# Hybrid decoder layer: the forgetting queries and keys as four pairs by seven products behind the heads, token-major values at the heads' seams

## The chip, the cores and the metric

The kernel runs on one core of a Trainium2 chip. The core's engines run side by side, each through its own list of instructions: TensorE (PE; its weight loads are PEld), VectorE (DVE), ScalarE (ACT), GpSimd (POOL), and SyncE (SP), on whose queue all DMAs are issued. The metric is the device time of one execution in microseconds (us).

## The reference, cut to what matters

The layer works on 1024 tokens of width 1024. A first normalisation is followed by one wide projection, whose columns feed two groups of heads: four mLSTM heads (queries and keys through a causal convolution, values, an output gate, two scalar gates) and eight forgetting-attention heads (queries, keys, values, one gate). Then come cross-attention into 256 memory tokens and an MLP with a squared ReLU.

```python
h = rmsnorm(x, ln1[l])
z = h @ w_in[l]
ml_qk, ml_v, ml_o, ml_i, ml_f, fx_q, fx_k, fx_v, fx_f = jnp.split(z, splits, axis=-1)
ml_qk = jax.nn.silu(causal_conv(ml_qk, ml_conv_w[l], ml_conv_b[l]))
...
mh = mlstm_chunkwise(mq, mk, mv, ig, lf)
...
fx_out = forgetting_attention(fq, fk, fv, flf).reshape(B, S, FX_W)
x = x + jnp.concatenate([ml_out, fx_out], axis=-1) @ w_out[l]
x = x + cross_attention(...)
...
```

The part that the change rewrites is `fx_q` and `fx_k`: h (1024 tokens by 1024) times 512 columns of weights for the queries and 512 for the keys.

## The kernel before, in words

**Number format.** Every matrix product is made in float32 by three matmuls (`mm3`, lines 186 to 188): each operand is cut into a high and a low part by `split` (lines 134 and 135: a ScalarE copy for the high part, a VectorE subtraction for the low one; lines 137 and 138 where a factor goes in), and low times high, high times low and high times high add up in one bank.

**Order of the work.** The program is written stage after stage, but a planner lays out each engine's list: it takes the instructions by the order in which the program has them, passes over one whose operands or buffers are not there yet by its own estimate, and takes a later one instead. Tiles have names (`w2("p")` is the name `r_p`, `act`, `w4`, `z4`, `wr` for raw weights, `wh` and `wl` for cut ones; `sc`, `tp`, `mm`, `m2`, `ov` for the eight banks of PSUM) and a number of buffers each: act 7, w4 5, z4 2, wr 2, wh and wl 3, r_p 2, r_c 2; sc 3, tp 2, the others 1. `mm()` gives out banks by the list `banks`. Where an order is wanted exactly, `in_order()` chains the instructions of an engine; the attention's slots do so.

**The stages that matter here.**
1. `first_values` makes the first half of the mLSTM values together with the gates while x arrives. The squares' sums (line 234) give the factors `rcol` of the norm; `first_sink` evicts the banks with them (lines 138 and 379).
2. `token_major(a["w_mv"], mv_sink, (1,), ...)` makes the second half of the values in eight tiles of 128 tokens by 256 columns, 24 matmuls each. Among the tiles stand `row_first` (the factors as a row across the partitions, by a transpose at line 249 and two DMAs through `rowd`) and `gate_rows` (transposes at lines 457 and 462, scans at 463 and 467); `gate_cols` follows.
3. `ml_project(hd)` for each of the four mLSTM heads: `conv_silu` of the key (a projection of two halves of 24 matmuls into two banks, evicted with the norm row at line 507, four taps at lines 510 and 512, tanh at 514, the product at 515, in two `z4` tiles that line 505 begins); `fx_project(0, hd)`; the carried state (lines 535 to 549); `conv_silu` of the query; `fx_project(1, hd)`; the output gate `og` (line 672).
4. `fx_project(which, n)` is a plain projection: 128 columns of queries or keys, 48 matmuls of 128x512, evicted with the norm row (line 641), cut and stored to the scratch `fqk` (lines 644 and 645).
5. `ml_head(hd, ...)` is the head itself: scores into `sc`, weights by exp (line 586), mask (588), product (589), cut, and the value product into `ov`; its closing steps run as a generator (`closing`) between the steps of the next projection. Four heads follow one another; head 3 is the last.
6. Forgetting attention: `fx_load` loads a head's queries and keys from `fqk` into `stacks` (whose memsets are line 696); `slot` issues one step each of scores (lines 734 and 735), maximum, exp, scaling and value product. Thirteen slots of scores lead (`LEAD_`), and behind them `token_major(a["w_fv"], fv_sink, ...)` makes the forgetting values in 16 tiles. From then on each value slot also takes work from `filler()` (memory keys and values, the first part of the output projection), at `RATE` planned units a slot.

## Time and profile before

| what | value |
|---|---|
| device time, median of three runs | 1511.57 us (1509.03 to 1512.43) |
| profiled execution, first to last instruction | 1509.2 us (no other time of its own is given) |
| TensorE busy | 1493.0 us, 7806 matmuls |
| weight loads busy | 1263.7 us |
| VectorE busy | 1122.7 us |
| ScalarE busy | 757.7 us |
| GpSimd busy | 528.7 us |

The page gives for each engine the time in which it ran an instruction. Matmuls overlap their neighbours in these records, so that single durations are longer than the step from one to the next; a stretch of the span, divided by the matmuls in it, gives the step. A row of waits names the waiting instruction, what released it, the time in all, the number of times and the longest.

### The profile page before, as it was taken

How to read it: one execution, taken by the hardware profiler on the slowest of the kernel's cores; microseconds unless marked ns; L12 is line 12 of the kernel's file. 1: busy time of each engine (PE TensorE's matmuls, PEld its weight loads, DVE VectorE, ACT ScalarE, POOL GpSimd, SP SyncE). 2: the span in 40 equal slices, each digit the busy share in tenths (PEclk: the TensorE clock that was granted, in tenths of full speed). 3: DMA queues.
4: the chain of work that ended last, by engine and by line, in shares of the span. 5: the costliest groups of instructions: out<-in, count | busy, mean ns of one | idle time of the engine just before them, and what ended most of it. 6: DMA issues, size and time to landing. Idle time of an engine off the chain costs nothing.

```text
span 1509.2 us, 22358 instructions
## 1 busy us (share of the span) xinstructions
PE 1493.0 (99%) x7806; PEld 1263.7 (84%) x7806; DVE 1122.7 (74%) x1803; ACT 757.7 (50%) x1440; POOL 528.7 (35%) x545
## 2 busy tenths in 40 slices
PE   9999999999999999999999999999999999999997
PEld 9988888889899888788988878888888888888887
DVE  7766676664788875667767899989996678787765
ACT  7324343334688764566654467566664521122134
POOL 1003030414365441623300044454544365553312
PEclk9999999999999999999999999999999999999999
DMA  6322333435777877853354447676678677776623
GB/s 243 115 79 95 98 108 126 132 129 153 247 261 256 284 248 246 271 169 126 128 182 159 147 155 279 235 261 248 217 273 292 264 279 279 279 272 251 247 88 112
DMA packets 124276, 303.04 MB, mean 201 GB/s; under 512 B 13810, under 2 KB 28460, under 8 KB 117252
## 3 DMA queue, kind: packets, MB, share of 16 engines
q1 hardware_dynamic: 124164, 301.62, 57.3%
q8 instruction: 61, 1.00, 0.3%
q14 instruction: 51, 0.42, 0.1%
HBM read 202.75 MB, written 98.82 MB: 200 GB/s over the span
## 4 chain that ended last, share of the span: by engine, by line
PE 90%; DMA 4%; DVE 3%; ACT 1%; issue 1%; POOL 1%; POOLq 0%; DVEq 0%; SPq 0%; ACTq 0%
PE tp L186 8%; PE tp L187 8%; PE tp L188 8%; PE sc L186 6%; PE sc L188 6%; PE sc L187 6%; PE mm L186 5%; PE m L188 5%; PE m L186 5%; PE m L187 5%; PE mm L188 5%; PE mm L187 5%; PE ov L801 2%; PE ov L186 2%; PE ov L187 2%; PE ov L188 2%
## 5 line engine op out<-in xcount | busy, mean ns | idle before, releaser
L186 PE MATMUL tp<-act,wl 128*128 128x512 f32 (+1 forms) x440 | 172.6, 392 | 0.0
L187 PE MATMUL tp<-act,wh 128*128 128x512 f32 (+1 forms) x440 | 172.1, 391 | 0.0
L188 PE MATMUL tp<-act,wh 128*128 128x512 f32 (+1 forms) x440 | 171.8, 392 | 0.0
L135 DVE TENSOR_TENSOR wl<-wr,wh 128x1024 fp32r<-128x1024 f32 (+2 forms) x99 | 131.4, 1327 | 27.0 <-ACT wh L134 26.7
L134 ACT ACTIVATE wh<-wr 128x1024 fp32r<-128x1024 f32 (+2 forms) x99 | 99.8, 1008 | 85.7 <-PE tp L188 32.7
L186 PE MATMUL mm<-act,wl 128*128 128x512 f32 (+1 forms) x332 | 124.8, 376 | 2.6 <-DVE r_c L138 2.1
L188 PE MATMUL mm<-act,wh 128*128 128x512 f32 (+1 forms) x332 | 124.1, 374 | 0.0
L187 PE MATMUL mm<-act,wh 128*128 128x512 f32 (+1 forms) x332 | 123.8, 373 | 0.0
L186 PE MATMUL m<-act,wl 128*128 128x512 f32 (+1 forms) x308 | 113.8, 369 | 0.6 <-DVE wl L135 0.6
L188 PE MATMUL m<-act,wh 128*128 128x512 f32 (+1 forms) x308 | 113.8, 369 | 0.0
L187 PE MATMUL m<-act,wh 128*128 128x512 f32 (+1 forms) x308 | 113.7, 369 | 0.0
L188 PE MATMUL sc<-act,wh 128*128 128x512 f32 (+1 forms) x280 | 105.6, 377 | 0.0
L187 PE MATMUL sc<-act,wh 128*128 128x512 f32 (+1 forms) x280 | 105.6, 377 | 0.0
L186 PE MATMUL sc<-act,wl 128*128 128x512 f32 (+1 forms) x280 | 105.6, 377 | 0.0
L1612 POOL TENSOR_TENSOR z<-wr 128x256 f32<-128x256 f32 x56 | 52.9, 966 | 131.8 <-DMA wr<-w_ff2q 126.7
L188 PEld LDWEIGHTS tp<-act,wh 128*128 128x128 f32 x440 | 82.7, 188 | 19.0
L186 PEld LDWEIGHTS tp<-act,wl 128*128 128x128 f32 x440 | 82.7, 188 | 18.5
L187 PEld LDWEIGHTS tp<-act,wh 128*128 128x128 f32 x440 | 82.7, 188 | 18.2
L134 ACT ACTIVATE wh<-z 128x1024 fp32r<-128x1024 f32 (+1 forms) x54 | 55.5, 1027 | 81.8 <-POOL z L1612 62.3
L135 DVE TENSOR_TENSOR wl<-z,wh 128x1024 fp32r<-128x1024 f32 (+1 forms) x54 | 77.7, 1439 | 11.4 <-ACT wh L134 11.4
L134 ACT ACTIVATE w<-wr 128x768 fp32r<-128x768 f32 (+3 forms) x35 | 28.0, 801 | 107.4 <-PE tp L186 33.0
L186 PEld LDWEIGHTS mm<-act,wl 128*128 128x128 f32 x332 | 62.7, 189 | 14.2 <-DVE r_c L138 2.6
(734 smaller groups left out, 4387.2 us busy)
## 6 DMA issues: line engine op xcount, KB each, us to landing
act<-right SPq DMA_DIRECT2D x49, 1024.0 KB
right<-w SPq DMA_DIRECT2D x56, 256.0 KB
wr<-w_ff2q SPq DMA_DIRECT2D x28, 512.0 KB
right<-r_d SPq DMA_DIRECT2D x49, 256.0 KB
right<-r_e SPq DMA_DIRECT2D x49, 256.0 KB
act<-fqk SPq DMA_DIRECT2D x48, 256.0 KB
wr<-w_in SPq DMA_DIRECT2D x20, 512.0 KB
wr<-w_ff SPq DMA_DIRECT2D x20, 512.0 KB
```

The lines of the kernel that those rows point to most:

```text
L134: s.activation(hi, src, AF.Copy)
L135: return v.tensor_tensor(out=lo, in0=src, in1=hi.bitcast(F32), op=ALU.subtract)
L186: nc.tensor.matmul(ps, w[1], x[0], start=first, stop=False, skip_group_check=more)
L187: nc.tensor.matmul(ps, w[0], x[1], start=False, stop=False, skip_group_check=more)
L188: nc.tensor.matmul(ps, w[0], x[0], start=False, stop=last, skip_group_check=more)
L801: nc.tensor.matmul(self.ov[:, c0:], self.fv[:, self.j], t[:, c0:], start=self.j == 0 and t is self.p[1], stop=self.last and t is self.p[0])
L1612: g.tensor_tensor(out=o, in0=x, in1=y, op=op)
```

## The change

`fx_project` is gone from the heads' seams. The eight mLSTM value tiles of the second half and the 16 tiles of forgetting values, which stood ahead of the heads and behind the first scores, go there instead, four ahead of the carried state and four behind the query's convolution (`token_units`, called by `ml_project` for heads 1, 2 and 3; head 0 has none). `row_first` and `gate_rows` stand without tiles around them.

Behind the heads, the query and key projections are made as four pairs of one query tile and one key tile. Each pair is a 2 by 2 product of blocks (query and key columns by the two halves of the depth, against the two halves of the depth by the two halves of the tokens), made with seven block products in place of eight. Their right sides are four blocks or sums of blocks (`t1` to `t4`) of the normed input, made from x once by `first_rights` and `last_rights`, and the blocks of h themselves; the left sides are made from the weights by `left_in`. `InPair.run` makes a product (four k by three matmuls of 128x512) and evicts or adds, and stores to `fqk`. `in_jobs` is the order of the products. The query and key quarters of heads 0 and 2 (before: 1 and 3) now lie in an `act` tile.

In the attention's lead, the forgetting values are gone, and the slots take work from `filler()`, at `WARM` planned units a slot; `RATE` goes from 4.6 to 4.0.

```diff
--- before.py
+++ after.py
...
@@ -485,19 +488,17 @@
                 load(decay[sign, p_], cut[p_].bitcast(F32))
-    def token_major(w_src, sink, cs=(0, 1), between={}):
-
-        for c in cs:
-            ws = [both(weights(w_src[c, i]), lambda t: t.rearrange("p (k c) -> p k c", k=4)) for i in range(2)]
-            for t in range(8):
-                if t in between:
-                    between[t]()
-                hf, tt = divmod(t, 4)
-                ps = mm()[:, 0:256]
-                for k in range(KT):
-                    x = both(h[hf], lambda z: z[:, k, tt * P : (tt + 1) * P])
-                    mm3(ps, x, both(ws[k // 4], lambda z: z[:, k % 4]), k == 0, k == KT - 1)
-                sink(t, c, ps)
+    def token_units(w_src, sink, c):
+        ws = [both(weights(w_src[c, i]), lambda t: t.rearrange("p (k c) -> p k c", k=4)) for i in range(2)]
+        for t in range(8):
+            hf, tt = divmod(t, 4)
+            ps = mm()[:, 0:256]
+            for k in range(KT):
+                x = both(h[hf], lambda z: z[:, k, tt * P : (tt + 1) * P])
+                mm3(ps, x, both(ws[k // 4], lambda z: z[:, k % 4]), k == 0, k == KT - 1)
+            sink(t, c, ps)
+            yield
     def conv_silu(n, hi, lo):
         w = weights(a["w_in"][n])
@@ -634,16 +635,6 @@
     fqk = dram.tile([2, 2, 4, P, T], F32, name="fqk")
-    def fx_project(which, n):
-        w = weights(a["w_in"][12 + 4 * which + n])
-        for _, hf, ps in proj(w, h, 1):
-            lo = w2("p")
-            v.scalar_tensor_tensor(out=lo, in0=ps, scalar=1.0 if which else FXD ** -0.5, in1=row[:, hf * TH : hf * TH + TH], op0=ALU.mult, op1=ALU.mult)
-            hi = w2("p", dt=F32R)
-            split(hi, lo.bitcast(F32R), lo)
-            load(fqk[which, 0, n, :, hf * TH : hf * TH + TH], hi.bitcast(F32))
-            load(fqk[which, 1, n, :, hf * TH : hf * TH + TH], lo)
-
     fvd = dram.tile([FXH, P, 8, 2 * FXD], F32, name="fvd")
     def fv_sink(t, c, ps):
@@ -653,18 +644,20 @@
     closing = iter(())
-    def ml_project(hd):
-        qk = quarters(F32R) if hd % 2 else [w4(dt=F32R) for _ in range(4)]
+    def ml_project(hd, tiles=iter(())):
+        qk = quarters(F32R) if hd % 2 == 0 else [w4(dt=F32R) for _ in range(4)]
         q, k = qk[:2], qk[2:]
         weighed = weigh(hd)
         yk = conv_silu(MLH + hd, *k)
         next(closing, None)
-        fx_project(0, hd)
+        for _ in range(4):
+            next(tiles, None)
         next(closing, None)
         state = carried(hd, yk, *weighed)
         next(closing, None)
         yq = conv_silu(hd, *q)
-        fx_project(1, hd)
+        for _ in range(4):
+            next(tiles, None)
         sums = carry(hd, q, yq, *state)
         og = w4()
         for _, hf, ps in proj(weights(a["w_in"][8 + hd]), h, 1):
@@ -675,17 +668,187 @@
     banks[:] = ["tp", "m2", "tp", "sc", "mm", "sc", "sc"]
     turn[0] = 0
-    token_major(a["w_mv"], mv_sink, (1,), {2: row_first, 4: gate_rows})
+    row_first()
+    gate_rows()
     gate_cols()
     banks[:] = ["mm", "tp", "m2", "tp"]
     with tc.issue_after(last_sum.ins):
         mem_prepare()
+    mv_tiles = token_units(a["w_mv"], mv_sink, 1)
+    fv_tiles = [token_units(a["w_fv"], fv_sink, c) for c in range(2)]
     ready = ml_project(0)
     for hd in range(MLH):
         closing = ml_head(hd, *ready)
         next(closing)
         if hd < MLH - 1:
-            ready = ml_project(hd + 1)
+            ready = ml_project(hd + 1, (mv_tiles, *fv_tiles)[hd])
+    I_RIGHT = {}
+    for c, hf, k0 in (("11", 0, 0), ("21", 0, 4), ("22", 1, 4)):
+        I_RIGHT[c] = [both(h[hf], lambda t: t[:, k0 + k]) for k in range(4)]
+    raw_x = act(F32)
+    t1, t2 = act(), act()
+    I_RIGHT["t1"] = [(t1[:, k], t1[:, 4 + k]) for k in range(4)]
+    I_RIGHT["t2"] = [(t2[:, k], t2[:, 4 + k]) for k in range(4)]
+    I_RIGHT["t3"] = [both(h[1], lambda t: t[:, k]) for k in range(4)]
+    I_RIGHT["t4"] = [(t[:, :TH], t[:, TH:]) for t in (w4(dt=F32R) for _ in range(4))]
+    def gain(n):
+        return vec[:, VEC["ln1"] + n :][:, 0:1]
+    def x_part(k, hf, tag):
+        t = w2(tag)
+        load(t, a["x"][:, 4 + k, hf * TH : hf * TH + TH])
+        return t
+    def first_rights():
+        for hf in range(2):
+            load(raw_x[:, 4 * hf : 4 * hf + 4], a["x"][:, 0:4, hf * TH : hf * TH + TH])
+        for k in range(4):
+            x, y = raw_x[:, k], raw_x[:, 4 + k]
+            z = x_part(k, 1, "pc"[k % 2])
+            s.activation(y, y, AF.Copy, scale=gain(k))
+            v.scalar_tensor_tensor(out=x, in0=x, scalar=gain(k), in1=y, op0=ALU.mult, op1=ALU.subtract)
+            s.activation(I_RIGHT["t1"][k][0], x, AF.Copy, scale=-1.0)
+            v.scalar_tensor_tensor(out=I_RIGHT["t1"][k][1], in0=x, scalar=-1.0, in1=I_RIGHT["t1"][k][0].bitcast(F32), op0=ALU.mult, op1=ALU.subtract)
+            s.activation(z, z, AF.Copy, scale=gain(4 + k))
+            g.tensor_tensor(out=x, in0=z, in1=x, op=ALU.add)
+            sub(y, z, y, g)
+            split(*I_RIGHT["t3"][k], y)
+    def last_rights():
+        for k in range(4):
+            x = raw_x[:, k]
+            split(*I_RIGHT["t2"][k], x)
+            z = x_part(k, 0, "pc"[k % 2])
+            v.scalar_tensor_tensor(out=x, in0=z, scalar=gain(4 + k), in1=x, op0=ALU.mult, op1=ALU.subtract)
+            split(*I_RIGHT["t4"][k], x)
+    I_NAMES = {1: "11", 2: "21", 5: "t1", 6: "t2", 3: "22", 7: "t3", 4: "t4"}
+    i_cycle = ("sc", "mm", "tp", "sc", "m2", "tp", "sc", "ov")
+    def i_bank():
+        turn[0] += 1
+        return ps_tile(i_cycle[turn[0] % 8])
+    IP = 4
+    in_jobs = [(0, 1), (0, 5), (0, 2), (0, 3), (1, 1), (1, 5), (1, 2), (0, 6), (1, 3), (0, 7), (0, 4), (1, 6), (1, 7)]
+    for p_ in range(2, IP):
+        in_jobs += [(p_, 1), (p_ - 1, 4)] + [(p_, i) for i in (5, 2, 6, 3, 7)]
+    in_jobs.append((IP - 1, 4))
...
+    def left_in(p_, group):
+        if group == 0:
+            in_raws[p_] = [sb("wr", [P, 1024], 2) for _ in range(2)]
+            for raw, n in zip(in_raws[p_], (16 + p_, 12 + p_)):
+                load(raw, a["w_in"][n])
+        r2, r1 = in_raws[p_]
+        x11, x12, x21, x22 = r1[:, :TH], r1[:, TH:], r2[:, :TH], r2[:, TH:]
+        if group == 0:
+            t = z4()[:, :T].bitcast(F32R)
+            h22, l22 = t[:, :TH], t[:, TH:]
+            split(h22, l22, x22)
+            in_cuts[p_, 4] = both((h22, l22), lambda t: t.rearrange("p (k c) -> p k c", k=4))
+        hi, lo = (sb(t, [P, 1024], 3, F32R) for t in ("wh", "wl"))
+        split(hi, lo, (r1, r2, r1)[group])
+        if group == 0:
+            by = g if p_ else v
+            by.tensor_tensor(out=x21, in0=x21, in1=x22, op=ALU.add)
+            sub(x22, x21, x11, by)
+            sub(x12, x12, x22, by)
+            sub(x11, h22.bitcast(F32), x22, by)
+            by.tensor_tensor(out=x11, in0=x11, in1=l22.bitcast(F32), op=ALU.add)
+        for e in range(2):
+            in_cuts[p_, ((1, 2), (5, 6), (7, 3))[group][e]] = both((hi, lo), lambda t: t[:, e * TH : e * TH + TH].rearrange("p (k c) -> p k c", k=4))
+    class InPair:
...
+        def run(self, i, l):
+            r = I_RIGHT[I_NAMES[i]]
+            at_ = {1: "a", 2: "a", 5: "c", 3: "c", 6: "b", 7: "b", 4: "b"}[i]
+            if i in (1, 5, 6):
+                setattr(self, at_, i_bank())
+            ps = getattr(self, at_)
+            for k in range(4):
+                mm3(ps, both(l, lambda t: t[:, k]), r[k], i in (1, 5, 6) and k == 0, k == 3, True)
+            u = self.u
+            if i == 1:
+                self.p1 = w2("p")
+                s.activation(self.p1, ps, AF.Copy)
+            elif i == 2:
+                v.tensor_tensor(out=self.room("11", "a", "y"), in0=ps, in1=self.row_of("11"), op=ALU.mult)
+                self.done("11")
+            elif i == 5:
+                self.add(self.room("22", "e"), ps, self.p1)
+            elif i in (6, 3):
+                if "12" not in u:
+                    self.add(self.room("12", "b", "f"), ps, self.p1)
+                else:
+                    self.add(u["12"], ps, u["12"])
+                    self.scale("12")
+            elif i == 7:
+                self.add(u["22"], ps, u["22"])
+                self.scale("22")
+            elif i == 4:
+                u["21"] = self.p1
+                self.add(u["21"], ps, u["21"])
+                self.scale("21")
+        def scale(self, c):
+            g.tensor_tensor(out=self.u[c], in0=self.u[c], in1=self.row_of(c), op=ALU.mult)
+            self.done(c)
+        def done(self, c):
+            n, hf = int(c[0]) - 1, int(c[1]) - 1
+            x, at_ = self.u[c], slice(hf * TH, hf * TH + TH)
+            hi, lo = w2("d", dt=F32R), x.bitcast(F32R)
+            split(hi, lo, x, None if n else FXD ** -0.5)
+            load(fqk[n, 0, self.i, :, at_], hi.bitcast(F32))
+            load(fqk[n, 1, self.i, :, at_], x)
...
+    CLOSINGS = ((0, 2), (1, 1), (1, 2))
+    LEAD_IN = 5
+    first_rights()
+    last_rights()
+    for at, (p_, i) in enumerate(in_jobs):
+        while in_prep and in_first[in_prep[0]] <= at + LEAD_IN:
+            left_in(*in_prep.pop(0))
+        pair = in_open.setdefault(p_, None) or InPair(p_)
+        in_open[p_] = pair
+        pair.run(i, in_cuts.pop((p_, i)))
+        if i == 4:
+            del in_open[p_]
+        if (p_, i) in CLOSINGS:
+            next(closing, None)
     row_m = row[:, :NM]
     to_row(row_m, rcol_m, 2, rowd[1:2, :NM])
@@ -1085,25 +1248,24 @@
     fx_load(1)
     while coming:
         fx_step()
-    for i in range(LEAD_):
-        slot(False, 0)
-        if i in (1, 11):
-            next(closing, None)
-    token_major(a["w_fv"], fv_sink, between={4: lambda: next(closing, None)})
     hm = act().rearrange("p a b -> p (a b)").rearrange("p (e k c) -> p e k c", e=2, k=KT)
     load(hm.bitcast(F32), hmd)
     banks[:] = ["mm", "m2"]
     raw_load()
     raw_load()
-    RATE, DELAY = 4.6, 3
+    WARM = 6.0
+    for i in range(LEAD_):
+        slot(False, max(i - 1, 0) * WARM)
+        if i == 0:
+            cut_for(0)
+    base = spent[0]
+    RATE, DELAY = 4.0, 3
     n = 0
-    while slot(True, max(n - DELAY, 0) * RATE):
+    while slot(True, base + max(n - DELAY, 0) * RATE):
         n += 1
-        if n == 2:
-            cut_for(0)
     while adds or late or ended or stores:
         n += 1
-        slot(False, (n - DELAY) * RATE)
+        slot(False, base + (n - DELAY) * RATE)
     now[2] = True
     for step in fill:
         cut_next()
...
```

23 lines of the change are left out of this document (21 added, 2 removed).

## The prediction

> **What bounds the kernel now.** I read the page first (busy shares), then what TensorE waited for, then stretches of the span one by one.
>
> ```profile
> span 1509.2 us, 22358 instructions
> PE 1493.0 (99%) x7806; PEld 1263.7 (84%) x7806; DVE 1122.7 (74%) x1803; ACT 757.7 (50%) x1440; POOL 528.7 (35%) x545
> ```
> ```profile
> PE mm L186 <- DVE r_c L138: 2.1, 1, 2.1
> PE ov L129 <- POOL ident L118: 1.9, 1, 1.9
> PE mm L213 <- DVE c_r L1754: 1.6, 1, 1.6
> PE sc L734 <- ACT act L756: 1.6, 3, 1.1
> PE m L186 <- DVE wl L135: 0.6, 1, 0.6
> PE sc L1748 <- POOL r_b L226: 0.5, 1, 0.5
> PE sc L734 <- ACT w L756: 0.4, 1, 0.4
> PE mm L186 <- DVE wl L135: 0.4, 1, 0.4
> PE tp L782 <- DVE r_b L138: 0.4, 1, 0.4
> ```
> ```profile
> core 0: us, PE busy (x) PEld busy (x) DVE busy (x) ACT busy (x) POOL busy (x), PEclk, DMA share, GB/s
> 173.20:178.80 5.60, 5.60 (x26) 4.51 (x24) 3.03 (x4) 1.06 (x1) 0.00 (x0) 1.00 0.22 50
> 260.10:329.50 69.40, 69.40 (x337) 57.74 (x336) 46.78 (x73) 26.50 (x44) 19.51 (x21) 1.00 0.40 132
> 329.50:358.70 29.20, 29.20 (x232) 28.62 (x231) 14.51 (x30) 12.58 (x27) 13.76 (x16) 1.00 0.46 143
> 642.46:645.88 3.42, 3.42 (x11) 2.65 (x10) 2.59 (x4) 2.10 (x4) 0.00 (x0) 0.50 0.87 287
> ```
>
> TensorE is the bound, almost without a hole: the waits (in all, times, longest) sum to 9.5 us, and none of their lines is one of the heads'. So the time is the number of matmuls times their pitch plus whatever holes open. The pitch of a 128x512 matmul is in the row 173.20:178.80, one half of a projection: 24 matmuls (26 are counted with the neighbours that the edges cut) in 5.60 us, 0.233 us each. The holes are closed because the planner puts projections and token tiles into the heads' latencies. The change must be judged by both: how many matmuls go, and which holes lose their filler.
>
> **Removed: 48 matmuls.** `fx_project` ran eight times, 2 halves x 24 matmuls: 384. Four pairs of seven products, 4 k x 3 each: 336. 48 x 0.233 = 11.2 us less. The 24 token tiles (8 of the second values, 16 of the forgetting values) stay as they are, in other places. This is the whole gain: **-11.2 us**.
>
> **Beside it.** Off TensorE the pairs swap 16 evictions (L641) and 16 cuts for five evictions, four cuts and the weights' cuts per pair:
>
> ```profile
> 330.31 0.69 DVE L641 SCALAR_TENSOR_TENSOR r_p<-mm,row 128x512 f32<-128x512 f32 x1 [1.80 <-DMA fqk<-r_p]
> L1339 POOL TENSOR_TENSOR z<-z,z x14: 1290/1304/1686, 885.0 to 1130.8; 128x512 f32<-128x512 f32 x14
> ```
>
> VectorE: 10 x 0.69 + 3 x 1.22 = 10.6 us for a pair that lasts 84 x 0.233 = 19.6 us; GpSimd: 8 x 1.3 = 10.4 us (five on the left sides, three scalings). Both fit. `first_rights` and `last_rights` add about 24 VectorE and 32 ScalarE passes of 0.7 us and 4 MB on SP's queue (two loads of 1 MB, eight of 256 KB); at the DMA share of 0.40 and VectorE's 47 of 69 us in the stretch of a head there is room. SP's stores of `fqk` stay 32. All this at nothing; if the cover went, VectorE would delay an eviction by single passes of 0.7 us. At heads 1 to 3 the seams keep their length: 8 tiles x 24 matmuls of 256 columns stand where 96 matmuls of 512 stood.
>
> **Part A, the start.** Up to now the second values filled 34 to 61 us while the norm row and the gates were made, and the four `fx` halves of head 0 filled the conv's latency. Now neither is there. Which work may step in is limited by the buffers:
>
> ```profile
> 34.51 1.22 DVE L370 TENSOR_TENSOR w<-w,w 128x1024 f32<-128x1024 f32 x1
> 39.04 1.84 PE L234 MATMUL ov<-ones,w 128*128 128x1 f32 x16
> 42.60 0.16 DVE L208 SCALAR_TENSOR_TENSOR rcol<-c_t,c_y 128x4 f32<-128x4 f32 x1
> 45.30 0.23 DVE L379 TENSOR_SCALAR w<-mm,rcol 128x16 f32<-128x16 f32 x1
> 49.62 0.60 PE L462 MATMUL tp<-ident,w 128*4 128x128 f32 x4
> 53.45 0.26 DVE L441 SCALAR_TENSOR_TENSOR w<-w 128x96 f32<-128x96 f32 x1
> 54.21 0.60 PE L457 MATMUL sc<-ident,w 128*12 128x128 f32 x4
> 54.64 0.60 PE L462 MATMUL sc<-ident,w 128*4 128x128 f32 x4
> 55.50 2.28 DVE L463 TENSOR_TENSOR_SCAN act<-w,act 12x1024 f32<-12x1024 f32 x1 [0.60 <-ACT act L458]
> 65.67 1.21 DVE L138 SCALAR_TENSOR_TENSOR w<-act,w 12x1024 fp32r<-12x1024 f32 x1
> 86.32 0.10 POOL L505 MEMSET z<- 128x3 f32 x1 [10.68 <-DVE z L515]
> ```
>
> L462 transposes the input gates, ready at 45.5. Its `tp` tile went at 49.62, its `sc` tile only at 54.64, right behind L457's `sc` tile, which the program asks for first and whose input (L441) was not ready before 53.7. So tiles of one name are given out in the order of the program; only other names may pass. Now `gate_rows` asks for tp, m2, tp, sc, and head 0's key conv then for mm (first half) and tp. The mm bank is free after L379 of the last first-values tile; the tp tile stands behind the gates'. Times after: the sums (L370) end at 35.7 as before, rcol 3.7 us later (39.04 to 42.76), mm free 2.8 us after that, at 42.2. There the first half runs, 5.6 us, to 47.8. The gates' log-sigmoid ends 8.2 us after the bank (45.5 to 53.7), about 50; the second half runs about 51 to 57, then the first half of the query conv on mm, to 62. Its second half waits in tp behind the carried state; mm waits for the query's `z`, whose buffer (two of that name) comes free with the key conv's L515, as L505 shows at 86.32. That chain after 57 us:
>
> ```profile
> L507 DVE TENSOR_TENSOR z<-tp,row x8: 672/692/692, 68.3 to 299.1; 128x512 f32<-128x512 f32 x8
> L510 DVE TENSOR_SCALAR z<-z,vec x8: 811/813/1304, 76.9 to 307.2; 128x1024 f32<-128x1024 f32 x8
> L512 DVE SCALAR_TENSOR_TENSOR z<-z,vec,z x24: 1269/1278/1758, 78.8 to 312.8; 128x1024 f32<-128x1024 f32 x24
> L514 ACT ACTIVATE z<-z x8: 1058/1060/1063, 83.9 to 314.2; 128x1024 f32<-128x1024 f32 x8
> L515 DVE SCALAR_TENSOR_TENSOR z<-z,z x8: 1209/1218/1224, 85.0 to 316.7; 128x1024 f32<-128x1024 f32 x8
> ```
>
> 0.69 + 0.81 + 3 x 1.28 + 1.06 + 1.22 = 7.6 us, so 64 to 65 with VectorE free. But the gates' scans, sums and cuts come first: from L463 at 55.50 to L138's end at 66.9, 11.4 us in the trace, seven passes of gate work with three others among them. Begun at 51 they end at 62; where the taps wait for them some 4 us are lost: 69. From 34.1 to 69 are 34.9 us; TensorE has 3 x 5.6 = 16.8 us of conv and about 6 us of sums and transposes. **A costs 12 us**; between 6 (VectorE yields at once) and 18 (the chain at its end, 75, if other weights' cuts push in).
>
> **Part B, head 3 and the pairs.** Head 3's latency was filled with forgetting values. Now these lie at its own seam, ahead of it, and the filler is the pairs. But `t2` needs a seventh `act` buffer: four hold h, `raw_x` and `t1` have two, and the last is the values' `mv[1]`, read until head 3's last value product. Pair 0's copy of product 1 (`r_p`, two buffers) stands behind the four x parts of that name, of which the third is released only after `t2`'s first cut. So (0,2), product 2 of pair 0, and all behind it wait for head 3, and of the pairs only (0,1) and (0,5), 2 x 12 x 0.233 = 5.6 us, can fill.
>
> ```profile
> 329.52 0.40 PE L186 MATMUL sc<-act 128*128 128x512 f32 x1
> 350.08 3.66 POOL L696 MEMSET act<- 32x2048 f32 x2
> 355.28 0.43 DVE L135 TENSOR_TENSOR r_e<-r_c,r_d 128x256 fp32r<-128x256 f32 x1
> 358.35 0.28 PE L188 MATMUL ov<-r_d,act 128*128 128x256 f32 x1
> 371.60 1.94 DMA facd<-r_a
> 373.56 5.12 DMA r_a<-facd
> ```
>
> Before, head 3 takes 29.2 us from its first score to its last value product, with 7.7 us of its own matmuls (2 halves x 2 x 3 of 512, 384, 256, 256 columns) and 0.9 of sums. About 8 us of the 29.2 need not recur: the POOL memsets (3.7) that stood ahead of its last mask, 2.4 us in which the last product was ready (L135's end at 355.7) but queued, 1.8 us of VectorE on an `fqk` store (L641 above). Left 21.3, less 8.6 and 5.6: 7 us of hole. Then the `t2` cut, the x part and the copy: four passes of 0.7 us less a microsecond of sums, 2 us. **B costs 9 us**; 5 to 17 (nothing of the 8 saved). Behind that the pairs run without a hole: their order needs `t2`'s last part some 12 us later, `t4` 25.
>
> **Part C, the first scores.** Before, 2.4 us of waits fall there (L734 and L782 above). Now memory-key units, up to 6 planned units a slot, stand in for the forgetting values; the first one's eviction needs `row_m`, which waits for the pairs' last scaling and two DMAs. The nearest row of that shape is `facd`, written and read back: 1.9 + 5.1 = 7 us; the first key unit is 24 matmuls of 256 columns, some 3 us at half the pitch above, with scores ahead of it, so 1 or 2 us may stay. I take 0, between -2.4 (the old waits gone) and +4.
>
> **Part D, the clock.** After the one hole above 2 us within the work (2.1 us before 641.74) the row 642.46:645.88 shows a granted clock of 0.50 for 3.42 us: 1.7 us lost. A has two holes above that size, B one. Nearest row: 1.7 us each; I take two, **3.4 us**; 0 to 7. [...]
>
> **Sum.** -11.2 + 12 + 9 + 0 + 3.4 = +13.2 on the profiled execution's span of 1509.2: 1522.4. The page gives no time around the span; the three runs' median, 1511.57, stands 2.4 above it: 1524.8, **1525 us**.
>
> **Rivals.**
> 1. *Faster: the holes are filled.* If the planner grants buffers out of order, or reaches the pairs' later products during head 3, A falls to about 2 and B to 2: -11.2 + 4 = -7, 1504. For it: not one hole over 1.2 us through the heads now. Against: the `sc` transposes at 54.64. It decides from A + B + D below 11. Chance 0.20.
> 2. *Nothing comes of it:* A 6, B 5, D 0 and C 0 give 0: 1511.5. Chance 0.12 for within 0.2% (3 us), about what a measurement of this kernel can tell from no change.
> 3. *Worse:* A 18, B 15, D 7, C 2: +31, 1542. For it: VectorE's gate work is serial and first in line. Chance 0.10.
> 4. [...] Chance 0.08.
> The forecast, +4 to +25, has the remaining 0.50.
>
> Forecast, 3 and 4 are slower: 0.68; same 0.12; faster 0.20. The range reaches half into the rivals: 1503 to 1537; the forecast's own is 1515 to 1536.
>
> **What would show it.** Right: TensorE idle 10 us or more in 34 to 75, ended by mm's eviction, then by the key conv's `z`; the first product (0,2) only after head 3's last value product, with a hole of 5 us or more ahead; 48 matmuls fewer; granted clock 0.50 behind these holes. Wrong: waits of TensorE that stay near 10 us in all would mean rival 1; a hole spread over the pairs would mean that weights or GpSimd set their pace, which I put at nothing.

## The result, and the profile after

The changed kernel takes 1577.5 us (median of four runs, 1575.6 to 1578.3) where the kernel before takes 1512.0 beside it: a ratio of 1.0436, interval 1.0421 to 1.0451, or 65 us more. The forecast of "slower" held; 1525 and the range's end of 1537 did not. The page after:

```profile
span 1575.3 us, 22436 instructions
PE 1513.1 (96%) x7758; PEld 1272.2 (81%) x7758; DVE 1172.2 (74%) x1848; ACT 778.5 (49%) x1476; POOL 591.1 (38%) x580
```

There are 48 matmuls fewer (7806 to 7758), and yet TensorE is busy 20.1 us longer. At 0.233 us each the 48 should have saved 11.2, so about 31.3 us of busy time come from somewhere else: most of it from the clock, as shown below. The other 46 us are idle time (span less PE busy: 16.2 before, 62.2 after). TensorE's longest waits after, in all, times, longest; before, all of them summed to 9.5 us with none of the heads' lines among them:

```profile
PE tp L189 <- DVE r_b L791: 6.0, 1, 6.0
PE m L190 <- DVE wl L1152: 4.8, 1, 4.8
PE sc L536 <- DVE c_m L532: 4.6, 1, 4.6
PE sc L189 <- DVE wl L135: 3.9, 4, 1.2
PE mm L189 <- DVE w L382: 3.4, 1, 3.4
PE ov L237 <- ACT emc L483: 2.8, 1, 2.8
```

(L189 to L191 are the three matmuls of `mm3` now; L382, L536 and L483 belong to the start, L791 is a pair's eviction, L1152 the cut of the weights that `filler()` uses.) Stage by stage, after: behind the bounds stand the length, the busy times of PE, PEld, DVE, ACT and POOL (with their instructions), the granted clock, and the share and rate of the DMA. The stages are the start, heads 0, 1 and 2 (with the projections for the next head), head 3, the pairs, the first scores, and the rest:

```profile
34.10:104.20 70.10, 56.20 (x269) 45.94 (x268) 48.88 (x82) 21.82 (x37) 4.42 (x7) 0.85 0.27 82
104.20:170.30 66.10, 64.27 (x388) 56.73 (x387) 38.58 (x64) 22.95 (x41) 14.82 (x16) 0.97 0.16 49
170.30:246.25 75.95, 73.23 (x434) 64.77 (x433) 54.41 (x86) 32.78 (x58) 16.77 (x20) 0.96 0.46 146
246.25:320.80 74.55, 71.89 (x434) 63.77 (x433) 50.15 (x81) 29.18 (x53) 18.29 (x18) 0.98 0.29 89
320.80:349.00 28.20, 23.00 (x97) 18.74 (x95) 17.68 (x26) 13.29 (x26) 15.46 (x18) 0.76 0.26 80
349.00:439.50 90.50, 81.52 (x328) 63.85 (x328) 65.95 (x87) 32.64 (x55) 60.31 (x40) 0.92 0.56 187
439.50:466.00 26.50, 19.59 (x132) 18.48 (x132) 14.47 (x37) 12.51 (x33) 10.45 (x12) 0.87 0.65 220
466.00:773.00 307.00, 302.97 (x1776) 261.80 (x1775) 232.58 (x535) 213.04 (x538) 138.48 (x187) 1.00 0.68 229
773.00:1575.30 802.30, 788.36 (x3677) 646.27 (x3675) 624.88 (x807) 372.57 (x592) 309.15 (x251) 1.00 0.61 220
```

The same from head 3 to the end before:

```profile
329.50:392.80 63.30, 61.89 (x493) 60.34 (x492) 35.51 (x87) 28.14 (x68) 22.50 (x28) 1.00 0.57 180
392.80:700.00 307.20, 304.07 (x1794) 264.43 (x1793) 229.23 (x527) 209.14 (x528) 137.22 (x185) 0.99 0.70 235
700.00:1509.20 809.20, 799.45 (x3770) 658.26 (x3769) 633.43 (x826) 383.07 (x615) 313.24 (x255) 1.00 0.61 220
```

Length less busy gives the idle time: 13.9 us in the start, 7.2 in heads 0 to 2, 5.2 in head 3, 9.0 in the pairs, 6.9 in the first scores, 18.0 in the rest. Before, it was none at all from 34.1 us up to head 3, then 1.4, 3.1 and 9.8. Four of the stretches in which the granted clock was 0.50 (half clock, below):

```profile
38.49:48.73 10.24, 5.71 (x15) 4.64 (x16) 8.29 (x27) 4.64 (x12) 1.02 (x1) 0.50 0.51 185
69.22:79.46 10.24, 5.59 (x19) 4.93 (x20) 6.80 (x13) 2.72 (x4) 1.77 (x2) 0.50 0.24 88
205.75:212.58 6.83, 5.87 (x20) 5.20 (x21) 3.68 (x12) 2.14 (x6) 1.65 (x1) 0.50 0.81 231
335.45:355.93 20.48, 18.15 (x62) 14.84 (x61) 12.63 (x21) 9.87 (x20) 8.24 (x10) 0.50 0.12 34
```

In all the record has 77.9 us at half clock, against 12.1 before (the end of the program, some 9 us, among both). TensorE was busy for 53.0 us of it after and 3.5 before. A 128x512 matmul follows the one before it by 0.43 us there (369.53 to 372.94 after) where 0.233 is the step at 1.00, so about half of the difference, some 25 us as an estimate, is what the clock can have added to the busy time. The other 6 or 7 of the 31.3 are no clock: a 128x512 matmul that nothing follows at once is recorded with its full 0.40 us where the step in a row of them is 0.233, and TensorE's busy time falls into 46 pieces after, 12 before. An estimate from these: 34 x 0.17 = 6 us. The longest stretch lies on head 3: TensorE is "busy" 18.2 of its 20.5 us, mostly with that head's own narrow matmuls, and the clock is back at 1.00 only from 355.93, behind the first matmuls of the dense product that began at 352.6.

### The profile page after: what moved, and what is told of

Same layout as the page of the kernel before. It is cut to its first block, busy times and chain, and to the rows that moved or that the text cites. A ratio compares the mean times of both kernels' runs of the same rounds, so it can differ in the third digit from the quotient of the medians.

```text
span 1575.3 us, 22436 instructions
## 1 busy us (share of the span) xinstructions
PE 1513.1 (96%) x7758; PEld 1272.2 (81%) x7758; DVE 1172.2 (74%) x1848; ACT 778.5 (49%) x1476; POOL 591.1 (38%) x580
## 4 chain that ended last, share of the span: by engine, by line
PE 72%; DVE 12%; DMA 6%; ACT 4%; issue 3%; POOL 2%; SPq 0%; DVEq 0%; POOLq 0%; ACTq 0%
PE tp L189 6%; PE tp L190 6%; PE tp L191 6%; PE sc L189 5%; PE sc L190 5%; PE sc L191 5%; PE mm L189 4%; PE mm L190 4%; PE mm L191 4%; PE m L190 4%; PE m L189 4%; PE m L191 4%; DVE wl L135 3%; PE ov L964 2%; PE tp L945 2%
## 5 line engine op out<-in xcount | busy, mean ns | idle before, releaser
L135 DVE TENSOR_TENSOR wl<-wr,wh 128x1024 fp32r<-128x1024 f32 (+2 forms) x103 | 137.6, 1337 | 29.8 <-ACT wh L134 29.1
L189 PE MATMUL tp<-act,wl 128*128 128x512 f32 (+1 forms) x372 | 148.5, 400 | 6.8 <-DVE r_b L791 6.0
L190 PE MATMUL tp<-act,wh 128*128 128x512 f32 (+1 forms) x372 | 148.3, 399 | 0.0
L191 PE MATMUL tp<-act,wh 128*128 128x512 f32 (+1 forms) x372 | 147.3, 397 | 0.0
L189 PE MATMUL mm<-act,wl 128*128 128x512 f32 (+1 forms) x328 | 124.8, 381 | 7.3 <-DVE w L382 3.4
L189 PE MATMUL sc<-act,wl 128*128 128x512 f32 (+1 forms) x332 | 125.5, 378 | 3.9 <-DVE wl L135 3.9
L191 PE MATMUL sc<-act,wh 128*128 128x512 f32 (+1 forms) x332 | 124.8, 376 | 0.0
L190 PE MATMUL sc<-act,wh 128*128 128x512 f32 (+1 forms) x332 | 124.8, 376 | 0.0
L191 PE MATMUL mm<-act,wh 128*128 128x512 f32 (+1 forms) x328 | 123.0, 375 | 0.0
L189 PE MATMUL m<-act,wl 128*128 128x512 f32 (+1 forms) x288 | 107.6, 374 | 0.0
L190 PE MATMUL m<-act,wh 128*128 128x512 f32 (+1 forms) x288 | 107.3, 373 | 0.0
L191 PE MATMUL m<-act,wh 128*128 128x512 f32 (+1 forms) x288 | 107.3, 372 | 0.0
L1770 POOL TENSOR_TENSOR z<-wr 128x256 f32<-128x256 f32 x56 | 48.8, 891 | 126.9 <-DMA wr<-w_ff2q 114.1
L134 ACT ACTIVATE w<-wr 128x768 fp32r<-128x768 f32 (+3 forms) x35 | 28.1, 803 | 129.0 <-PE mm L189 47.7
L189 PEld LDWEIGHTS tp<-act,wl 128*128 128x128 f32 x372 | 70.9, 191 | 24.3 <-DVE r_b L791 6.4
L191 PEld LDWEIGHTS tp<-act,wh 128*128 128x128 f32 x372 | 70.9, 191 | 16.6
L190 PEld LDWEIGHTS tp<-act,wh 128*128 128x128 f32 x372 | 70.9, 190 | 16.5 <-DVE act L135 0.4
L189 PEld LDWEIGHTS mm<-act,wl 128*128 128x128 f32 x328 | 63.0, 192 | 19.6 <-DVE w L382 3.5
```

The source lines that it names most:

```text
L134: s.activation(hi, src, AF.Copy)
L135: return v.tensor_tensor(out=lo, in0=src, in1=hi.bitcast(F32), op=ALU.subtract)
L189: nc.tensor.matmul(ps, w[1], x[0], start=first, stop=False, skip_group_check=more)
L190: nc.tensor.matmul(ps, w[0], x[1], start=False, stop=False, skip_group_check=more)
L191: nc.tensor.matmul(ps, w[0], x[0], start=False, stop=last, skip_group_check=more)
L1770: g.tensor_tensor(out=o, in0=x, in1=y, op=op)
```

## The experiments

The kernels ran in sets, each beside runs of the kernel before, whose medians differ by up to 2 us from set to set. So across sets the ratios to the kernel before are compared; a difference of ratios times 1511.6 gives the us.

### Which part of the change costs what

**e3**, plain projections in the pairs' place:

```
-    (rights, pairs, in_jobs ...)
+    for n in range(4):
+        for which in range(2):
+            fx_project(which, n)
+            if n < 2: next(closing, None)
```

> The changed kernel, with the forgetting queries and keys as eight plain projections of 48 matmuls (384) behind the heads instead of four pairs by seven products (336); the token tiles stay where the change has them. Theory (what head 3 lacks is work that may start: the products wait for buffers that head 3 holds, a plain projection for none but r_p): the plain projections fill head 3, so the holes between 329 and 369 us (11 us), the pairs' 3 us and 27 us of half clock (worth some 11) go against 11.2 us of matmuls more: 1577 - 14 = 1563 us. Rival (the place behind the heads is at fault, not the form): the holes of head 3 stay, and the time is 1577 + 11 = 1588 us less at most 3.

1544.0 us, ratio 1.0225 (1.0210 to 1.0240): 32 us below the change by the ratios, with 48 matmuls more. The theory's direction holds, at more than twice its size: there is no hole over 0.4 us between 282 and 423 us, and no half clock there.

**e2**, another buffer for the forgetting values:

```
-        o = rotate("b", "p", "c").bitcast(F32R)...
+        o = rotate("p").bitcast(F32R)...
```

> The changed kernel, with the forgetting values' evictions into the two r_p buffers alone instead of r_b, r_p and r_c in turn. Theory (the evictions queue in program order behind the running head's own r_b and r_c tiles, so the banks stay taken and the filler stops): of the 7.2 us of holes in heads 1 to 3's projections (104 to 321 us) those at 203 to 207 and at 280 to 283 us, 5.4 us, go, and with them 10.2 us of half clock, worth 4 to 5: 1577 - 9 = 1568 us. Rival (the filler has simply run out there): 1575 to 1580 us, the holes at the same places.

1563.1 us, ratio 1.0352 (1.0335 to 1.0369). The trace shows it on the first such tile of head 1's stretch. After the change its last matmul, then its eviction:

```profile
190.19 0.28 PE L191 MATMUL mm<-wh,act 128*128 128x256 f32 x1
205.29 0.47 ACT L137 ACTIVATE r_b<-mm,rcol 128x256 fp32r<-128x256 f32 x1 [1.05 <-PE sc L220]
```

In e2:

```profile
189.39 0.28 PE L191 MATMUL mm<-wh,act 128*128 128x256 f32 x1
190.84 0.47 ACT L137 ACTIVATE r_p<-mm,rcol 128x256 fp32r<-128x256 f32 x1
```

The `mm` bank stood full for 14.8 us before its eviction began, because r_b is given out in the program's order and head 1's sum of weights (read by L220) still held it; in e2 it waits 1.2 us. That the filler stops for want of free banks is argued from this; the holes at 203 to 207 and 280 to 283 us, and the 10.2 us of half clock behind them, are gone. It gained 12.7 us by the ratios where 9 were expected.

**e15**, e3 and e2 together:

> e3's kernel (all plain, behind the heads) with the forgetting values' evictions in r_p alone. Theory (e2's gain came from the projections of heads 2 and 3, whatever stands behind them): 1544 - 8 = 1536 us, the holes at 202 to 207 and 281 us gone. Rival (e2's 14 us came from head 3's end, which plain projections fill anyway): 1542 us or more.

1536.8 us, ratio 1.0166 (1.0146 to 1.0185): 9 below e3 by the ratios, as the theory has it; the holes up to 132 us are the only ones left before the first scores.

**e13 and e14** bring back the start, and plain projections for pairs 0 and 1 in heads 0 and 1:

```
+    for i, _ in enumerate(token_units(a["w_mv"], mv_sink, 1)):
+        if i == 1: row_first()
+        if i == 3: gate_rows()
...
+        if hd < 2: fx_project(0, hd)     # and (1, hd) in the second place
...
-            ready = ml_project(hd + 1, (mv_tiles, *fv_tiles)[hd])
+            ready = ml_project(hd + 1, ((), *fv_tiles)[hd])
```

> The start and the projections of heads 0 and 1 as in the kernel before (second values at the start, plain forgetting projections of pairs 0 and 1 in the two places of heads 0 and 1), forgetting values in r_p at heads 2 and 3's projections, and only pairs 2 and 3 as seven products behind the heads (24 matmuls, 5.6 us, fewer than before); memory's norm row in columns 512 to 767. Theory (what the change lost before head 3 it lost by taking filler from the start and the seams; what it lost behind, by the products' waits): the holes and half clock before 320 us go, those of head 3 and of the products' start stay, some 5 + 6 us and 10 us of half clock: 1511 - 5.6 + 21 + 2 = 1528 us. Rival (the losses before head 3 come from the forgetting values' place, not from the start): holes of 5 us and more before 320 us, 1540 us or more.

> As e13, but pairs 2 and 3 also as plain projections behind the heads (384 matmuls in all, as before the change). Theory (the seven products' price is the waits of head 3's end, whatever else is mended): 1511 to 1516 us, 12 us or more below e13, without a hole over 2 us between 320 and 400 us. Rival (work behind head 3 costs the same in any form): within 4 us of e13.

e14 takes 1517.3 us, ratio 1.0037 (1.0023 to 1.0050), with no hole above 0.42 us from the first value tile to the first scores; e13 takes 1551.6, ratio 1.0266 (1.0246 to 1.0286). On the same start, two pairs by seven products cost 35 us more than two pairs plain, though they spare 24 matmuls. e13's theory was right that nothing is lost before head 3 (no hole over 0.6 us there), but its 1528 us was 24 too low: what the products cost behind that point was put at half its size. e14's held, give or take 1 us. Pages of e14, e15 and e2:

```profile
span 1515.9 us, 22383 instructions
PE 1493.5 (99%) x7806; PEld 1261.2 (83%) x7806; DVE 1123.0 (74%) x1803; ACT 757.1 (50%) x1440; POOL 524.3 (35%) x545
```
```profile
span 1533.3 us, 22388 instructions
PE 1500.0 (98%) x7806; PEld 1267.3 (83%) x7806; DVE 1123.5 (73%) x1803; ACT 757.3 (49%) x1440; POOL 527.7 (34%) x545
```
```profile
span 1561.3 us, 22438 instructions
PE 1507.2 (97%) x7758; PEld 1267.4 (81%) x7758; DVE 1175.4 (75%) x1848; ACT 778.8 (50%) x1476; POOL 585.8 (38%) x580
```

This makes a ladder from before to after (ratio times 1511.6; idle and busy from the pages; fx are the forgetting queries and keys, fv the forgetting values). e14 and e13 also have the memory's norm row in other columns (e5, below), which the step to e15 takes back:

| step | us | TensorE idle | TensorE busy |
|---|---|---|---|
| before to e14: fx of pairs 2 and 3 behind the heads, fv ahead | +5.6 | +6.2 | +0.5 |
| to e15: start emptied, all fx behind | +19.5 | +10.9 | +6.5 |
| to e2: seven products for plain projections | +28.1 | +20.8 | +7.2, with 11.2 us of matmuls fewer |
| to after: fv evicted to r_b, r_p, r_c in turn | +12.7 | +8.1 | +5.9 |

So the seven products lose 39 us against the 11.2 that they spare, on top of the moves; and e13 loses 40 against 5.6 with half as many pairs. The starts differ, but the price does not go by the pair.

### What in the seven products costs

**e16, e17, e18** leave the sums of the right sides, of the left sides, and both out of e13:

```
-    first_rights()
-    last_rights()                                     # e16, e18
-            by.tensor_tensor(out=x21, in0=x21, ...)   # e17, e18: five passes
```

> e13's kernel (two pairs), with the right sides' sums left out: no x is loaded again, and t1 to t4 are read from the cut halves of h, so these products' results are not the reference's. The number of matmuls stays. Theory (the price of the form, 34 us between e14 and e13, is the right sides: their loads, sums and cuts hold back the products in head 3, and head 3's own chain is slowed by them on VectorE): most of it goes, 1515 to 1525 us, the half clock of 24 us in head 3's end falls under 7 us. Rival (the left sides' sums on GpSimd and the evictions set it): 1545 us or more.

> e13's kernel, with the left sides' sums left out: each weight's parts are cut as they are loaded (five passes a pair on GpSimd or VectorE fewer), so the products' results are not the reference's. Theory (the right sides are the price): 1545 to 1552 us. Rival (GpSimd's left sides are): 1535 us or less.

> e13's kernel, with both left out. What remains of the form is the order of the products, their evictions' sums and the scaling on GpSimd. Theory (nothing else costs): e14 less the 24 matmuls, 1517 - 5.6 = 1512, to 1518 us. Rival (the evictions' sums, which wait for each other's buffers, cost as much as the sides): 1525 us or more.

Ratios 1.0156 (1.0136 to 1.0176), 1.0245 (1.0227 to 1.0264) and 1.0138 (1.0122 to 1.0154): against e13's 40 us above before, 23.6, 37.0 and 20.9. The right sides cost 17 us; the left sides' 3 lie within what these runs can tell. e16 takes away the right sides' loads, passes and buffers at once, and so does not tell these apart. e17's forecast held; e16 took 1534.4 us, between its theory (1525 at most) and its rival; e18 took 1532.0, on the side of its rival: it still stands 15 us above e14, 21 with its 24 matmuls fewer. e13's longest wait and its head 3:

```profile
PE tp L189 <- DVE r_b L808: 6.9, 1, 6.9
```
```profile
320.00:346.79 26.79, 22.56 (x101) 17.80 (x100) 25.02 (x27) 13.77 (x22) 14.39 (x12) 1.00 0.44 136
346.79:370.68 23.89, 21.49 (x69) 17.64 (x70) 14.93 (x26) 11.01 (x22) 10.34 (x13) 0.50 0.12 34
```

VectorE is busy 25.0 of the 26.8 us ahead of head 3's middle, TensorE then goes to half clock for 23.9 us, and the hole of 6.9 us follows. In e16 half clock there is 3.4 us and the hole 0.6, though one of 2.6 us, ended by a weights' cut, stands ahead of it. What is left in e18 are holes of 2.0 and 3.4 us in the first scores and of 1.8 and 3.2 us behind 640 us, with 13.7 us of half clock behind them:

```profile
PE m L190 <- DVE wl L1156: 3.4, 1, 3.4
PE sc L189 <- DVE wl L135: 3.2, 1, 3.2
```

The second lies in a part of the kernel that the change does not touch, where cuts queue on VectorE; that the turn of the buffers stands elsewhere there was not tested.

**e6** and **e9** tried to mend the right sides, e6 on e2's kernel, e9 on e5's (below):

```
-            split(*I_RIGHT["t2"][k], x)  then t4's part, for each k
+            t2's four cuts at once; t4's parts behind product (0, 7)      # e6
-            z = x_part(k, 1, "pc"[k % 2])   and   x_part(k, 0, "pc"[k % 2])
+            z = x_part(k, 1, "p")           and   x_part(k, 0, "c")        # e9
```

> e2's kernel, with only t2's four cuts made at head 3's end; the four x parts that t4 needs, their subtractions and t4's four cuts (12 VectorE passes of 0.7 us with ScalarE's) come behind product 7 of pair 0, their x parts in r_c alone. Theory (the hole of 5.3 to 6 us in the pairs' first products is VectorE's queue: cuts of the right sides, head 3's factor and the evictions all fall there): the hole falls to 2 us or less and its half clock goes: 1563 - 5 = 1558 us. Rival (the hole is a wait for buffers that head 3's end releases): within 1 us of 1563, the hole where it was.

> e5's kernel, with the x parts of t1, t2 and t3 all in r_p, and those of t4 all in r_c, instead of r_p and r_c in turn for both. Theory (in e6 and after, the parts in r_c were loaded only when head 3's last weights and squares left r_c, so half of t2 was summed, on GpSimd, behind head 3, and pair 0's product 1 waited for r_p in the same way): the sums of t2 are ready before head 3 ends, product 2 of pair 0 runs inside head 3, the hole of 4.9 us behind head 3 falls under 2 us: 1558 - 7 = 1551 us. Rival (the hole is VectorE's own queue at that time: evictions, factor, cuts of t2 and weights): the hole stays at 3.5 us or more, 1556 us or more.

e6: 1568.6 us, ratio 1.0379 (1.0362 to 1.0396), slower than e2 and outside both of its forecasts. t4's passes still ran at 352 to 362 us, so the edit did not test VectorE's queue; a hole of 6.2 us now ended with head 3's factor (c_fac). e9: 1561.7, ratio 1.0334 (1.0316 to 1.0351) against e5's 1.0309: no gain, though what its theory expected of t2 came true. After the change, half of t2's sums waited for the r_c that head 3 held; in e9 they did not, in the two rows that follow (the change, then e9):

```profile
L716 POOL TENSOR_TENSOR act<-r_c,act x2: 1389/1630/1871, 351.0 to 357.1; 128x512 f32<-128x512 f32 x2
```
```profile
L716 POOL TENSOR_TENSOR act<-r_p,act x4: 1281/1506/1715, 312.9 to 329.7; 128x512 f32<-128x512 f32 x4
```

Product 2 of pair 0 ran inside head 3, and the hole behind it fell from 4.9 to 1.2 us; but holes of 3.9 us (head 3's own squares) and 3.4 us (a weights' cut at 380 us) opened.

### The first scores

**e5**, on e2's kernel:

```
-    row_m = row[:, :NM]
+    row_m = row[:, TH : TH + NM]
-    [(p_, i) for i in (5, 2, 6, 3, 7)]
+    [(p_, i) for i in ((5, 2, 6, 3, 7) if p_ < IP - 1 else (5, 6, 7, 3, 2))]
```

> e2's kernel (the changed kernel with the forgetting values' evictions in r_p alone), with the memory's norm row in columns 512 to 767 of the row tile instead of 0 to 255, and the last pair's products in the order 1, 5, 6, 7, 3, 2, 4, so that the row is free two products (5.6 us) before the pairs end. Theory (the 4.8 us hole in the first scores is VectorE waiting for the row's way to memory and back at the first key unit's sink, with the next weights' cut queued behind it): the hole goes, with a stretch of half clock of 3.4 us: 1563 - 6 = 1557 us. Rival (the weights themselves come late, because the pairs hold their raw buffers): the hole stays within a microsecond, 1561 to 1564 us.

1558.3 us, ratio 1.0309 (1.0294 to 1.0324), 6.5 below e2 by the ratios, as its theory has it. The hole of 4.8 us falls to 0.5; which of the two edits did it was not tested. In the change, the first key unit's sink (L1048, at 452.6 us) held VectorE for

```profile
  DMA row<-rowd: 4.1, 1
```

and L1152, the cut for which TensorE waited, stood behind it in VectorE's queue.

### The start and the dealing-out of the tiles

**e1** (second values at the start, the sixteen fv tiles four to a head), **e10** (on e9: four tiles at the start, then 2, 5, 6, 7), **e11** (the same on e15) and **e12** (4, then 2, 4, 4, 5, and 5 behind head 3's projections):

> The changed kernel, with the eight tiles of the second values back at the start (norm row behind the second tile, gates behind the fourth, as before) and the sixteen forgetting-value tiles spread over all four heads' projections, two in each of the two places of a head. Theory (the emptied start is what costs): the 13.9 us of TensorE's holes between 34 and 76 us go, and with them the two stretches of half clock from 38.5 and 69.2 us, 10.2 us each, worth some 5 us: 1577 - 19 = 1558 us. Rival (filler is short everywhere, and moving it only moves the holes): four tiles a head instead of eight open holes of 3 us and more in each head, and the time stays above 1570 us.

> e9's kernel, with the 24 token tiles (second values, then forgetting values) dealt out anew: four at the start (norm row behind the first, gates behind the second), two in head 0's projections, five, six and seven in those of heads 1 to 3, instead of none, none, eight, eight and eight. Theory (five tiles' time is all that the start lacked, and a head needs less than eight): the start's holes (13.9 us) and its 20 us of half clock (worth 5) go, and thinner heads give back 6 at most: 1551 - 13 = 1538 us. Rival (as in e1, the filler is short everywhere): a hole of 5 us or more at another head's end, 1547 us or more.

> e3's kernel (plain projections of 384 matmuls behind the heads), with the forgetting values' evictions in r_p alone and the token tiles dealt out as in e10. Theory (with the places mended, the seven products still cost more than their 11.2 us, since only plain projections fill head 3 and leave VectorE, GpSimd and the buffers free): 1544 - 8 - 15 = 1521 us, below e10 by 15 or so. Rival (what the products cost was mended in e5 and e9): e11 stands above e10 by 5 to 11 us.

> e10's kernel, with the tiles dealt out as four at the start, two, four, four and five in the projections of heads 0 to 3, and five behind head 3's projections, ahead of the pairs, so that they can run inside head 3. Theory (head 3's sparse chain alone on TensorE is what keeps the clock at half for 20.5 us, worth 10): the half clock there falls to 7 us or less, 1538 - 9 = 1529 us. Rival (four tiles a head are too few, and the holes move to heads 1 and 2): 1538 us, within 3.

1580.0, 1575.7, 1539.4 and 1580.6 us; ratios 1.0462 (1.0447 to 1.0478), 1.0434 (1.0416 to 1.0451), 1.0186 (1.0169 to 1.0203), 1.0465 (1.0438 to 1.0493). None gained (against the kernels that they start from 4, 15, 3 and 5 us slower by the ratios): each closed holes in one place and opened them in another. In e1 the start has one hole left (1.4 us), and this one came, at head 3's output gate, whose buffer head 2's closing still held:

```profile
PE tp L189 <- DVE w L665: 12.5, 1, 12.5
```

e12's five tiles did run inside head 3, but pair 0's product 2 then waited 6.3 us for the copy of product 1 into r_p, and half clock in head 3 was still 13.7 us. The rivals of e1, e10 and e12 held in that nothing was gained. Of e11's theory the sign of the distance to e10 held (36 us instead of 15); its own time did not. Only e14, where the plain projections stand in heads 0 and 1 again, has heads without holes. So filler for start and heads is what the change gave away.

### The clock

**e4** on the change, **e7** and **e8** on the kernel before:

```
+                for _ in range(2 if hd == MLH - 1 and (hf or j) else 1):   # e4: the score's mm3
...
+            if now[1] in range(24, 84, 10):                                # e7, e8
+                scratch, ps = z4(), sc()
+                nc.tensor.matmul(ps[:, :P], ident, ident, ...)
+                s.activation(scratch[:, :P], ps[:, :P], AF.Copy)
+                g.memset(scratch[:, :1024], 1.0)     # twice; e8: 384 columns, once
+                nc.tensor.matmul(ps[:, :P], scratch[:, :P], ident, ...)
```

> The changed kernel, with every score of head 3 but the first computed twice (21 matmuls of 256 to 512 columns more, about 3.1 us of TensorE at full clock, thrown away). Theory (half clock follows a stretch of 3.4 us in which TensorE was busy for about half or less, and head 3's own sparse matmuls then hold it for 20.5 us): the stretch before 335 us is filled above that, the clock stays at 1.00 longer, and the time falls by 3 to 8 us: 1569 to 1574. Rival (half clock costs little because head 3 waits for its chain anyway): the extra matmuls lie in the holes, 1576 to 1580 us.

> The kernel before, with six stalls put into the values' stage (slots 24, 34, 44, 54, 64, 74): TensorE does one small matmul, ScalarE copies its result into a free buffer, GpSimd writes that buffer twice (1024 columns, about 1.8 us each), and TensorE does another small matmul on it, with the order of all engines kept; the results are thrown away. Each stall should be 4 to 5 us of idle TensorE. Theory (a hole of this size costs itself and then half clock for one or two stretches of 3.4 us): 1511 + 6 x 4.5 + 6 x (1.7 to 3.4) = 1548 to 1558 us, six stretches at 0.50 or more. Rival (the clock falls only where long sparse work follows): no half clock there, 1538 us.

> As the run with stalls of 4 us, but GpSimd writes 384 columns once (about 0.7 us), so that each of the six stalls is about 1.4 us of idle TensorE. Theory (half clock needs a stretch of 3.4 us in which TensorE is busy for little more than half or less): no half clock, 1511 + 6 x 1.4 = 1519 us. Rival (each hole of a microsecond or more halves the clock): 1511 + 8.4 + 6 x 1.7 = 1530 us.

e4: 1574.7 us, ratio 1.0436 (1.0415 to 1.0456), the change's own: 3.1 us of extra matmuls cost nothing measurable, and half clock in head 3 falls from 20.5 to 13.7 us; whether it gained can't be told, because its trace also has a hole of 4.0 us at 930 us, where the change has 2.4, with 6.8 us of half clock behind it. e7: 1548.2, ratio 1.0246 (1.0231 to 1.0261); e8: 1530.9, ratio 1.0128 (1.0113 to 1.0143). e7's six holes were 3.1 to 4.3 us (21.3 in all), and five of them were followed by half clock (20.5 us). e8's were 1.6 to 2.7 us (12.0 in all), and only the longest was. e7's time and stretches are its theory's. e8's time is its rival's 1530, but by luck: the rival had half clock behind every hole, and the holes came out at 2.0 us on average where 1.4 were meant. Three of e7's, in stretches of 3.41 us (in the change, half clock before the program's end lasts 3.41, 6.83, 10.24 or 20.48 us at a time, multiples of that length); the PEclk column is the first number behind the last bracket:

```profile
411.11:414.52 3.41, 0.27 (x4) 0.08 (x2) 1.60 (x3) 1.78 (x6) 3.35 (x5) 1.00 0.11 37
414.52:417.93 3.41, 3.41 (x13) 3.22 (x14) 0.82 (x2) 0.26 (x2) 0.21 (x2) 0.50 0.78 222
486.20:489.61 3.41, 1.49 (x14) 1.29 (x12) 1.89 (x5) 2.19 (x6) 2.10 (x4) 1.00 0.94 333
489.61:493.03 3.42, 1.67 (x14) 1.68 (x15) 0.81 (x3) 0.00 (x0) 1.64 (x2) 1.00 0.64 223
493.03:496.44 3.41, 3.41 (x28) 3.17 (x27) 1.60 (x4) 2.74 (x6) 0.99 (x2) 1.00 0.15 57
```

And two of e8's:

```profile
411.64:415.05 3.41, 1.81 (x12) 1.46 (x12) 1.66 (x4) 2.18 (x7) 2.60 (x6) 1.00 0.02 8
500.39:503.80 3.41, 0.69 (x7) 0.50 (x5) 2.34 (x6) 1.53 (x5) 2.66 (x4) 1.00 0.96 344
503.80:507.21 3.41, 3.41 (x14) 3.03 (x14) 0.76 (x2) 0.00 (x0) 0.00 (x0) 0.50 0.90 284
```

In e8 a hole of 2.7 us inside one stretch (500.39:503.80, busy 0.69 us) was followed by 3.41 us at 0.50; in e7 one of 3.7 us (ended at 491.36) that lies in two stretches, busy 1.49 and 1.67 us, was followed by none. So the clock's cost of one hole here, as an estimate from these rows, is 1.7 us or none, and 3.4 where half clock lasted 6.83 us, as in the change at 205.75:212.58 (busy 2.45 us in the first 3.41 of it). Both kernels cost 5 to 6 us more than holes and clock explain; the twelve small matmuls are among that, the rest was not traced.

## Why the prediction was right and wrong

Its sum against the trace (spans 1509.2 and 1575.3; the measured column is idle time after less before, from the rows above, but for the matmuls, which are reckoned at 0.233 us each, and the last two terms, which share out the busy time that is left):

| term | predicted | measured |
|---|---|---|
| 48 matmuls fewer | -11.2 | -11.2 |
| A, holes of the start | 12 | 13.9 |
| B, holes of head 3 and the first products | 9 (7 + 2) | 11.2 (5.2 + 6.0) |
| heads 0 to 2, "keep their length" | 0 | 7.2 |
| pairs behind their first hole, "without a hole" | 0 | 3.0 |
| C, first scores | 0 | 5.5 |
| the rest of the kernel | 0 | 5.1 |
| D, half clock | 3.4 | about 25 |
| longer records of matmuls ahead of holes | no term | about 6 |
| sum | 13.2 | 66.0 |

**A was right** in mechanism, and in its holes within 2 us: `mm` came free behind L382's eviction, and the gates and the key conv's chain ended the later holes. That chain ended at 75 us and not at 69, which is the forecast's own worse case; a part of the delay went into matmuls at half clock (44 to 48.7 us) and not into holes.

**B was right in its first part only; that its sum came near is luck.** Head 3 did lack filler (5.2 us idle where 7 were forecast), and product 2 of pair 0 did begin behind head 3's last value product, at 352.6 us, though the 2 us put ahead of it were 0.7 of idle time. The 6.0 us stand behind products 2, 3 and 6 of that pair, ahead of its product 7, and end with no buffer that head 3 holds. They are VectorE's queue, which the forecast put at nothing: VectorE was busy for the whole hole (DVE is the third of the busy times),

```profile
362.06:368.08 6.02, 0.00 (x2) 0.00 (x1) 6.02 (x11) 2.19 (x4) 3.16 (x3) 0.84 0.23 87
```

and of its passes these two evicted products 3 and 6, the second of which product 7 waited for:

```profile
365.60 0.68 DVE L791 TENSOR_TENSOR r_b<-tp,r_p 128x512 f32<-128x512 f32 x1
367.35 0.68 DVE L791 TENSOR_TENSOR r_b<-tp,r_b 128x512 f32<-128x512 f32 x1
```

Head 3 had its part in it by another way than the forecast's: half of t2's sums waited for x parts in r_c, which head 3 held, so VectorE stood idle for 1.9 us and then had the passes all at once:

```profile
359.68 1.10 DVE L135 TENSOR_TENSOR act<-act,act 128x512 fp32r<-128x512 f32 x1 [1.85 <-ACT act L134]
```

In e9, where these sums come earlier, the hole there is 1.2 us.

**D failed**, by some 21 us. The prediction counted two holes at 1.7 us each, from a single stretch. The price of one hole was about right (e7: 20.5 us of half clock behind five holes, about 2 us lost by each); the number and the length of the stretches were not. And the estimate missed that the clock stayed at 0.50 through head 3's narrow matmuls, busy as TensorE was: 20.5 us after the change (18.15 busy), 23.9 in e13 (21.49 busy). TensorE's busy time in the page grows by it.

**"Beside it" failed** twice. The heads' seams did not "keep their length": 12.7 us with the half clock there (e2). It compared the matmuls of the heads' places and found them equal; it did not ask into which buffers the moved tiles are evicted, though it used that rule, one name in the program's order, for B. And that VectorE fits was an average over a pair, with an eviction late "by single passes of 0.7 us" at worst: in the hole above, product 3's last matmul had ended by 362.1 us and its eviction began at 365.6, 3.5 us later, product 6's 5.3 us later. Passes for the right sides fall together with weights' cuts and head 3's own there; in e13 VectorE was busy 25.0 of 26.8 us ahead of head 3's middle, and without the right sides 17 us go (e16).

**C was sized too low.** The wait for the row's two transfers was foreseen; that a weights' cut stood behind the waiting sink on VectorE was not. The holes there grew by 5.5 us where 4 was the bound; e5 puts that wait at 6.5 us with its half clock.

Rival 1 fell at once: the planner did not fill the holes, and no other dealing-out of the tiles (e1, e10, e12) did. No kernel tried beats the one before; the nearest, e14, is 0.4% above it, and it has no seven products.

**Open:** of the form's 39 to 40 us, 17 are the right sides (how much of it by VectorE's queue and how much by their buffers was not told apart) and 3, at most, the left; about 20 were located (first scores, behind 640 us) but not traced to one cause each.

## What to carry to other kernels

Where TensorE is full and its holes are closed by filler, ask of an edit which filler it makes unusable, by buffers too, before counting the matmuls that it spares: 11 us of matmuls here stood against 39 us of waits and clock, and two pairs paid as much as four. Sum idle time and half clock as terms of their own: beside a chain of narrow matmuls one hole was followed by 20.5 us at half clock here. Ask of a helping engine not whether its passes fit on average but what stands ahead of the next eviction in its queue. When tiles move, follow their evictions to the buffers' names and ask who holds these at that time.
